# First weight chunk multiplied half by half, and three small tables given out at the second compressor chunk

## The chip, the cores and the metric

One core of a Trainium2 chip runs the whole program. The metric is the device time of one execution in microseconds (us). Its engines are TensorE (PE, with its weight loads PEld), VectorE (DVE), ScalarE (ACT), GpSimd (POOL) and SyncE (SP); each takes its instructions strictly in the order in which they were built, and waits on semaphores for the others and for transfers (DMA).

## The reference

Two decoder layers over 256 tokens of width 1024. Each layer normalises, makes one wide input projection, feeds two mixers and projects back onto the residual:

```python
def hybrid_layer(x, norm_g, w_in, ...):
    h = rms_norm(x, norm_g)
    z = h @ w_in
    (rg_x, rg_gate, q, k_c, v_c, k_s, v_s, k_w, v_w, nsa_gate, br_gate) = jnp.split(z, cuts, axis=-1)
    y_a = rg_lru(causal_depthwise_conv(rg_x, conv_w, conv_b), ..., rg_lam) * jax.nn.silu(rg_gate)
    y_b = nsa(q, k_c, v_c, k_s, v_s, k_w, v_w, br_gate, q_g, k_g, ...) * jax.nn.silu(nsa_gate)
    return x + jnp.concatenate([y_a, y_b], axis=-1) @ w_out

def rg_lru(x, w_r, b_r, w_i, b_i, lam):
    ...
    log_a = (-RG_C * r) * jax.nn.softplus(-lam)
```

The softplus of `lam` does not depend on the input x; the kernel makes it once for both layers, as a small table.

## The kernel before

Every product is done in three passes for precision: a weight chunk `raw` is split into a rounded high part `wh` (on ACT, `split`, line 167) and the rest `wl` (on DVE, line 170); the activations are likewise `hh` and `hl`. `mm3` (lines 175 to 177) adds high by high, then the two mixed products, into one PSUM bank. A product needs the chunk's `wh` for line 175's part and `wl` for one of the other two.

The weights come in chunks, in a fixed order. For layer 0: chunks 0 to 7 are `wt` (queries, and the keys of two branches; 768 columns, one eighth of the inner dimension each), chunks 8 and 9 `wc` (the compressor's keys and values), chunks 10 to 12 `wv` (values and gates), chunk 13 the first of twelve `wf`, then `wo`. SP issues the load of chunk n+4 when the subtraction that reads chunk n's `raw` buffer is done (four `raw` buffers), and SP takes its transfers in order: behind the `raw` of chunk 12 stand four small and large loads (`pes`, `w2s`, `rws`, and `yy`, which is two MB of `w1`), and behind these the `raw` of chunk 13. Chunk 0 alone is loaded and split in two halves of 384 columns; its first half is rounded on DVE (line 165), its second on ACT.

`tm1` multiplies chunk k by both token halves t and both column halves e: four PSUM banks (three named `s`, one `pp`), three matmuls each. In the same steps `first_x` scales x into `hh` and `hl` for that k, adds up squares (`sq_add`), loads the constants `cst` and the gains `ga` (k = 2), has POOL make rotary tables `cg`, `sg` from them (`tables2`, lines 247 to 252, at k = 4), has DVE copy an identity and a mask to bf16 (k = 4), and makes the `softplus` table (k = 5): two ACT operations and some seventeen small DVE operations of 128x8, of which lines 196 to 206 are one chain, each reading what the one before wrote (line 202 stands seven times).

After chunk 7, `rms1` turns the squares into the scale `rc` (PE line 310, DVE lines 311 to 320, a power on POOL, line 181) and sends it across partitions as `rp` by four tiny transfers; `cmp_scale` (ACT, line 443) needs `rp`, and the transposes of `cmp_in` (PE, line 449) need `cmp_scale`. `norm_sums` (ACT line 338, DVE lines 340 to 343, POOL line 181) and `norm_rope` (DVE lines 352 to 367) work on the two token halves. `v_out` (ACT lines 406 and 409) reads what the `wv` chunks made. Later `cmp_act` makes `hs` (line 477), which PE reads at lines 482 and 483.

The code gives instructions out in the order of the main loop; the framework's scheduler then sets each engine's order by when its own model finds them ready, so that an instruction can stand earlier or later on its engine than the code gives it out.

Of the kernel before, what the change touches and what calls it, by code (L numbers as in the profile page):

```python
# [18 lines left out]
P = 128  # L19
# [4 lines left out]
NT = S // P  # L24
# [47 lines left out]
def hybrid_trunk_kernel(ctx: ExitStack, tc: tile.TileContext, vx, wc, wt, wv, wf, wo, w1, w2, pe,  # L72
# [6 lines left out]
    V, A, G, T = nc.vector, nc.scalar, nc.gpsimd, nc.tensor  # L79
# [32 lines left out]
    for n in range(8):  # L112
        T.matmul(wb.rearrange("p (a s) -> p a s", a=2), wz[:, :P], wz[:, None].to_broadcast([P, 2, S]),
                 start=n == 0, stop=n == 7)
# [7 lines left out]
    def cview(n, p0=0, p1=P):  # L122
        a, b = CONST_COLS[n]
        return cst[p0:p1, a:b]

    ident = cview("ident")
# [5 lines left out]
    identb = cp.tile([P, P], BF16, name="identb")  # L132
    maskb = cp.tile([P, P], BF16, name="maskb")
# [40 lines left out]
    def mm3(o, lh, ll, rh, rl, start, stop):  # L174
        T.matmul(o, lh, rh, start=start, stop=False)  # L175
        T.matmul(o, lh, rl, start=False, stop=False)  # L176
        T.matmul(o, ll, rh, start=False, stop=stop)  # L177
# [12 lines left out]
    def softplus():  # L190
        sp = cp.tile([P, 6, DEPTH, 4], F32, name="sp")
        a, b = VEC_COLS["lam"]
        lam = vec[:, :, a:b]
        A.activation(sp[:, 0], lam, AF.Abs)
        A.activation(sp[:, 0], sp[:, 0], AF.Exp, scale=-1.0)
        V.tensor_scalar(sp[:, 1], sp[:, 0], 2.0, None, op0=ALU.add)
        V.reciprocal(sp[:, 1], sp[:, 1])
        V.tensor_tensor(sp[:, 1], sp[:, 1], sp[:, 0], op=ALU.mult)
        V.tensor_tensor(sp[:, 2], sp[:, 1], sp[:, 1], op=ALU.mult)
        V.tensor_scalar(sp[:, 3], sp[:, 2], 1.0 / 17, None, op0=ALU.mult)  # L200
        for c in (15, 13, 11, 9, 7, 5, 3):
            V.scalar_tensor_tensor(sp[:, 3], sp[:, 3], 1.0 / c, sp[:, 2], op0=ALU.add, op1=ALU.mult)
        V.scalar_tensor_tensor(sp[:, 3], sp[:, 3], 1.0, sp[:, 1], op0=ALU.add, op1=ALU.mult)
        V.tensor_scalar(sp[:, 4], lam, -4.0, 0.0, op0=ALU.mult, op1=ALU.max)
        V.scalar_tensor_tensor(sp[:, 4], sp[:, 3], 8.0, sp[:, 4], op0=ALU.mult, op1=ALU.add)
        V.tensor_scalar(sp[:, 5], sp[:, 4], -1.0, None, op0=ALU.mult)
        hb = cp.tile([P, DEPTH, 8], F32, name="hb")
        a = VEC_COLS["br"][0]
        V.tensor_scalar(hb, vec[:, :, a:a + 8], 0.5, None, op0=ALU.mult)
        return sp[:, 4], sp[:, 5], hb  # L210
# [5 lines left out]
    def h_split(l, h, k):  # L216
        A.activation(h[0][:, k], x_sb[:, k], AF.Copy, scale=v(l, "g", k))
        V.scalar_tensor_tensor(h[1][:, k], x_sb[:, k], v(l, "g", k), h[0][:, k].bitcast(F32),
                               op0=ALU.mult, op1=ALU.subtract)

    def sq_add(sq, k):
        if k == 0:
            A.activation(sq, x_sb[:, 0], AF.Square)
        else:
            sk = act([P, S], "tmp", 3)
            A.activation(sk, x_sb[:, k], AF.Square)
            V.tensor_tensor(sq, sq, sk, op=ALU.add)
# [4 lines left out]
    def tables(l):  # L232
        ga = act([P, NGAIN], "ga")
        nc.sync.dma_start(ga, gains[l:l + 1].to_broadcast([P, NGAIN]))
        return ga
# [22 lines left out]
    def layer(l, prev):  # L258

        L = Layer()  # L260
        steps = []

        def step(chunk, run, after=None, before=(), middle=()):
            steps.append((chunk, run, after, before, middle))
# [18 lines left out]
        def first_x(k):  # L283
            h_split(0, L.h, k)
            if k == 2:
                nc.sync.dma_start(cst, consts)
                L.ga = tables(0)
            if k == 4:
                V.tensor_copy(identb, ident)
                V.tensor_copy(maskb, cview("mask"))  # L290
                L.tabs = tables2(L.ga)
            for j in {2: [0], 3: [1, 2], 4: [3], 5: [4], 6: [5], 7: [6, 7]}.get(k, []):
                sq_add(L.sq, j)
            if k == 5:
                L.sp = softplus()

        def tm1(c, k):
            for t in range(NT):
                tok = slice(t * P, (t + 1) * P)
                for e in range(2):  # L300
                    mm3(L.acc1[t][e][:, :384], L.h[0][:, k, tok], L.h[1][:, k, tok],
                        c.hi[:, 0, e * 384:(e + 1) * 384], c.lo[:, 0, e * 384:(e + 1) * 384],
                        k == 0, k == KT - 1)
# [453 lines left out]
        F = lambda f, *a: (lambda: f(*a))  # L757
        R = lambda f, *a: (lambda c: f(c, *a))

        for k in range(KT):  # L760
# [8 lines left out]
            if l and k == 5:  # L769
# [2 lines left out]
        step(Chunk(wc[l, 0], 4, S), R(cmp_prod, 0), None, [small_loads, F(w1_load, 0), F(w1_load, 1), F(norm_sums, 0)],  # L772
             [F(norm_sums, 1)])
        step(Chunk(wc[l, 1], 4, S), R(cmp_prod, 4), cmp_scale, [],
             ([] if l else [rms2]) + [F(norm_rope, 0)])
        step(Chunk(wv[l, 0, :, :3], 3, 280), R(tm2, 0, 3), cmp_in, [],
             [F(norm_rope, 1)])
        step(Chunk(wv[l, 0, :, 3:6], 3, 280), R(tm2, 3, 3))
# [14 lines left out]
        for q in range(8):  # L793
            i, t = divmod(q, 2)
# [19 lines left out]
        for n, (kind, j) in enumerate(order):  # L814
            c = Chunk(wf[l, base[kind] + j], KT, P, dma=n >= 4)
# [14 lines left out]
    for l in range(DEPTH):  # L830
        prev, st_ = layer(l, prev)
        prev0 = prev0 or prev
        steps += st_
# [140 lines left out]
```

## Time and profile before

| what | us |
|---|---|
| median of the three timed runs | 248.19 (248.13 to 248.87) |
| the profiled execution, its own time | 248.74 |
| its span, first to last instruction | 247.0 |
| PE busy in the span | 240.0 |
| DVE busy | 195.2 |
| ACT busy | 163.7 |
| POOL busy | 44.5 |

The profile's rows give the start of an instruction, its length, its engine and line, what it writes and reads, and in square brackets the idle time before it with what ended it. A matmul's length covers a pipeline; the distance from one start to the next is what a matmul costs.

### The profile page before, as it was taken

Reading aid. Unit: us, or ns where it says so; the run is one execution under the profiler, and the core shown is the slowest. Engines: PE = TensorE matmul, PEld = TensorE weight load, DVE = VectorE, ACT = ScalarE, POOL = GpSimd, SP = SyncE. Lnnn points to the kernel's source line nnn. Section 1 sums busy time; section 2 is a strip of 40 time slices with the busy share of each in tenths; the row PEclk is TensorE's granted clock in tenths of the full one; section 3 lists DMA queues with packets and bytes.
Section 4 is the critical chain, followed back from the end, with each engine's and each line's share of the span. In section 5 each row is a group of like instructions: output and inputs, shape, how many; then the busy total and the mean of one; then the engine's idle time right before and its main releaser. Section 6 shows DMA issues by size and latency. Waiting matters only on the chain.

```text
span 247.0 us, 5194 instructions
## 1 busy us (share of the span) xinstructions
PE 240.0 (97%) x1950; PEld 222.1 (90%) x1950; DVE 195.2 (79%) x379; ACT 163.7 (66%) x414; POOL 44.5 (18%) x73
## 2 busy tenths in 40 slices
PE   8999998999999999999999999999999999999994
PEld 3999997978998899989999999987899979998993
DVE  5997698999999988654995559699997999865322
ACT  6965539799999878522872463778999998750100
POOL 0039660011600011000003044101100101110000
PEclk9999999999999999999999999999999999999998
DMA  6997999866799499842479978557669676860022
GB/s 214 363 294 268 330 404 396 261 230 170 231 338 385 129 272 323 245 150 61 133 243 328 331 247 253 183 170 239 194 189 352 220 257 165 292 226 2 3 85 85
DMA packets 17849, 57.17 MB, mean 231 GB/s; under 512 B 2464, under 2 KB 3616, under 8 KB 17312
## 3 DMA queue, kind: packets, MB, share of 16 engines
q1 hardware_dynamic: 12816, 39.86, 47.7%
q0 software_dynamic: 4864, 16.78, 21.7%
q8 instruction: 15, 0.25, 0.4%
q10 hardware_dynamic: 144, 0.20, 0.2%
q14 instruction: 10, 0.08, 0.1%
HBM read 55.78 MB, written 1.05 MB: 230 GB/s over the span
## 4 chain that ended last, share of the span: by engine, by line
PE 73%; DVE 13%; DMA 4%; ACT 3%; issue 2%; POOL 1%; SPq 0%; DVEq 0%; ACTq 0%
PE fm L175 14%; PE fm L177 13%; PE fm L176 13%; PE pp L627 4%; DVE wl L170 4%; PE s L175 3%; PE s L177 3%; PE s L176 3%; PE m L641 3%; DMA raw<-in_wv_dram 2%; PE s L587 2%; PE fm L670 2%; PE s L586 2%; DMA raw<-in_wt_dram 2%; DVE qs L390 2%
## 5 line engine op out<-in xcount | busy, mean ns | idle before, releaser
L170 DVE TENSOR_TENSOR wl<-raw,wh 128x1024 fp32r<-128x1024 f32 (+4 forms) x67 | 74.3, 1114 | 7.4 <-PE pp L176 2.4
L175 PE MATMUL fm<-hh,wh 128*128 128x256 f32 x192 | 56.9, 296 | 0.1
L177 PE MATMUL fm<-hh,wl 128*128 128x256 f32 x192 | 54.7, 285 | 1.0 <-DVE wl L170 1.0
L176 PE MATMUL fm<-hl,wh 128*128 128x256 f32 x192 | 54.6, 285 | 0.0
L167 ACT CAST wh<-raw 128x768 fp32r<-128x768 f32 (+4 forms) x34 | 30.4, 897 | 27.8 <-DMA raw<-in_wc_dram 7.8
L175 PEld LDWEIGHTS fm<-hh,wh 128*128 128x128 f32 x192 | 36.7, 191 | 1.9 <-issue 1.2
L177 PEld LDWEIGHTS fm<-hh,wl 128*128 128x128 f32 x192 | 36.7, 191 | 1.3 <-DVE wl L170 1.3
L176 PEld LDWEIGHTS fm<-hl,wh 128*128 128x128 f32 x192 | 36.7, 191 | 0.2
L599 ACT ACTIVATE pr<-s,sm 128x128 f32<-128x128 f32 (+1 forms) x64 | 26.2, 424 | 3.0 <-DVE sm L593 2.2
L175 PE MATMUL fm<-yy,wh 128*128 128x256 f32 x96 | 27.3, 285 | 0.0
L177 PE MATMUL fm<-yy,wl 128*128 128x256 f32 x96 | 26.8, 279 | 0.0
L176 PE MATMUL fm<-yy,wh 128*128 128x256 f32 x96 | 26.7, 279 | 0.0
L614 ACT ACTIVATE pr<-pr,sm 128x128 f32<-128x128 f32 (+1 forms) x64 | 23.9, 456 | 2.0 <-DVE sm L605 2.0
L156 POOL DMA_DIRECT2D wh<-in_wo_dram x16 | 8.5, 528 | 62.6 <-PE fm L177 22.6
L175 PEld LDWEIGHTS fm<-yy,wh 128*128 128x128 f32 x96 | 18.0, 188 | 0.8 <-issue 0.8
L177 PEld LDWEIGHTS fm<-yy,wl 128*128 128x128 f32 x96 | 18.0, 188 | 0.0
L176 PEld LDWEIGHTS fm<-yy,wh 128*128 128x128 f32 x96 | 18.0, 188 | 0.0
L156 POOL DMA_DIRECT2D wh<-in_wf_dram x16 | 8.8, 551 | 49.2 <-PE fm L177 22.8
L176 PE MATMUL s<-wl,hh 128*128 128x384 f32 x48 | 16.7, 348 | 0.2 <-DVE wl L170 0.2
L177 PE MATMUL s<-wh,hl 128*128 128x384 f32 x48 | 16.4, 341 | 0.0
L175 PE MATMUL s<-wh,hh 128*128 128x384 f32 x48 | 15.7, 351 | 0.0
L736 DVE TENSOR_TENSOR head<-head,fm 128x512 f32<-128x512 f32 x11 | 7.5, 686 | 9.8 <-PE fm L177 9.8
(207 smaller groups left out, 617.0 us busy)
## 6 DMA issues: line engine op xcount, KB each, us to landing
raw<-in_wf_dram SPq DMA_DIRECT2D x24, 512.0 KB, 5.1
wh<-in_wf_dram POOLq DMA_DIRECT2D x16, 512.0 KB, 5.3
raw<-in_wo_dram SPq DMA_DIRECT2D x16, 512.0 KB, 5.2
wh<-in_wo_dram POOLq DMA_DIRECT2D x16, 512.0 KB, 4.9
raw<-in_wt_dram SPq DMA_DIRECT2D x15, 384.0 KB, 4.0
yy<-in_w_dram SPq DMA_DIRECT2D x4, 1024.0 KB, 7.8
raw<-in_wc_dram SPq DMA_DIRECT2D x4, 512.0 KB, 5.3
raw<-in_wv_dram SPq DMA_DIRECT2D x4, 420.0 KB, 5.1
```

Source lines behind the costliest of these rows:

```text
L156: G.dma_start(self.wh, self.src)
L167: A.copy(hi[:, c], self.raw[:, c])
L170: V.tensor_tensor(lo[:, c], self.raw[:, c], hi[:, c].bitcast(F32), op=ALU.subtract)
L175: T.matmul(o, lh, rh, start=start, stop=False)
L176: T.matmul(o, lh, rl, start=False, stop=False)
L177: T.matmul(o, ll, rh, start=False, stop=stop)
L390: L.qk_done[t] = V.tensor_tensor(L.qs[HD:, g::2, tok], src, L.qs[:HD, g::2, tok].bitcast(F32), op=ALU.subtract)
L599: A.activation(pr[g][:, b], ov[:, b], AF.Exp, bias=sm[:, 0, 2 * g + b:2 * g + b + 1], accum_out=sm[:, 1, 2 * g + b:2 * g + b + 1])
L614: A.activation(pr[g][:, b], pr[g][:, b], AF.Copy, scale=sc_)
L627: T.transpose(pp[:, (2 * g + b) * P:(2 * g + b + 1) * P], pr[g][:, b, c * P:(c + 1) * P], ident)
L641: T.matmul(o[g * HD:(g + 1) * HD], L.vv[:, 0, b, g * HD:(g + 1) * HD], pt[:, g, b, 0:2].rearrange("p a s -> p (a s)"), start=h == b == 0, ...
L736: V.tensor_tensor(x_sb[:, m], x_sb[:, m], os_[0].rearrange("p (a s) -> p a s", a=2), op=ALU.add)
```

## The change

The products of chunk 0 are given out by column halves: for each half e, high by high for both token halves, then the `wl` products for both, then the `hl` products. Before, they went token half by token half, each with all three products of its two column halves. The bf16 identity, the mask and the softplus table, given out in the steps of chunks 4 and 5 before, are now given out by `small_tables` in the step of chunk 9, between its split and its products.

```diff
             if k == 4:
-                V.tensor_copy(identb, ident)
-                V.tensor_copy(maskb, cview("mask"))
                 L.tabs = tables2(L.ga)
...
-            if k == 5:
-                L.sp = softplus()
+
+        def small_tables():
+            V.tensor_copy(identb, ident)
+            V.tensor_copy(maskb, cview("mask"))
+            L.sp = softplus()
+
+
+        def tm1_first(c):
+            for e in range(2):
+                cols = slice(e * 384, (e + 1) * 384)
+                for q in range(3):
+                    for t in range(NT):
+                        tok = slice(t * P, (t + 1) * P)
+                        T.matmul(L.acc1[t][e][:, :384], L.h[q == 2][:, 0, tok], (c.lo if q == 1 else c.hi)[:, 0, cols],
+                                 start=q == 0, stop=False)
 
         def tm1(c, k):
+            if (l, k) == (0, 0):
+                return tm1_first(c)
...
-             ([] if l else [rms2]) + [F(norm_rope, 0)])
+             ([] if l else [rms2, small_tables]) + [F(norm_rope, 0)])
```

What the scheduler makes of it, at three places. All lines after 299 of the changed kernel have a number higher by 13.

On DVE, around the subtraction of chunk 7 (the last `wl` of 128x768). Before:

```order
L170 TENSOR_TENSOR wl<-raw,wh 128x768
L202 SCALAR_TENSOR_TENSOR sp<-sp 128x8
L227 TENSOR_TENSOR pct<-pct,tmp 128x256
L202 SCALAR_TENSOR_TENSOR sp<-sp 128x8
L203 SCALAR_TENSOR_TENSOR sp<-sp 128x8
L205 SCALAR_TENSOR_TENSOR sp<-sp 128x8
L206 TENSOR_SCALAR sp<-sp 128x8
L170 TENSOR_TENSOR wl<-raw,wh 128x768
L170 TENSOR_TENSOR wl<-raw,wh 128x1024
L311 TENSOR_SCALAR rc<-m 128x2
```

Now:

```order
L227 TENSOR_TENSOR pct<-pct,tmp 128x256
L294 CAST identb<-cst 128x128
L295 CAST maskb<-cst 128x128
L202 SCALAR_TENSOR_TENSOR sp<-sp 128x8 x6
L203 SCALAR_TENSOR_TENSOR sp<-sp 128x8
L205 SCALAR_TENSOR_TENSOR sp<-sp 128x8
L206 TENSOR_SCALAR sp<-sp 128x8
L170 TENSOR_TENSOR wl<-raw,wh 128x768
L324 TENSOR_SCALAR rc<-m 128x2
L170 TENSOR_TENSOR wl<-raw,wh 128x1024
```

The first seven or so operations of the table keep their early places; six of the seven at line 202 now stand in one row behind the subtraction of chunk 6 and ahead of that of chunk 7, where before four of them stood further up (three of these ahead of chunk 4's subtraction). The first operation on `rc` has moved ahead of chunk 8's subtraction.

On DVE, after the subtraction of chunk 9 (the second `wl` of 128x1024), where `norm_sums` reduces the squares `pt` to the sums `st`. Before:

```order
L170 TENSOR_TENSOR wl<-raw,wh 128x840
L340 TENSOR_REDUCE st<-pt 128x12 x2
L342 TENSOR_SCALAR st<-st,rc 128x8
L343 TENSOR_SCALAR st<-st,rc 128x4
L342 TENSOR_SCALAR st<-st,rc 128x8
L343 TENSOR_SCALAR st<-st,rc 128x4
L170 TENSOR_TENSOR wl<-raw,wh 128x840
```

Now:

```order
L353 TENSOR_REDUCE st<-pt 128x12
L170 TENSOR_TENSOR wl<-raw,wh 128x840
L355 TENSOR_SCALAR st<-st,rc 128x8
L356 TENSOR_SCALAR st<-st,rc 128x4
L353 TENSOR_REDUCE st<-pt 128x12
L170 TENSOR_TENSOR wl<-raw,wh 128x840
L355 TENSOR_SCALAR st<-st,rc 128x8
L356 TENSOR_SCALAR st<-st,rc 128x4
```

The sums of the first token half are finished ahead of the second half's reduction. On ACT the squares (line 338, now 351) stand between the casts of chunks 8, 9 and 10 where before all but the first stood behind that of chunk 10, and the first `vv` copy (line 406, now 419) stands ahead of the cast of chunk 13, where before it stood behind.

On DVE, where `hs` is made for the compressor. Before:

```order
L382 TENSOR_TENSOR kl<-pp,kd_122 64x2x128
L662 SCALAR_TENSOR_TENSOR cx<-xpad_72,head,cx 128x256
L390 TENSOR_TENSOR qs<-pp,qs 64x4x128
L477 SCALAR_TENSOR_TENSOR hs<-hth,m 128x160
L170 TENSOR_TENSOR wl<-raw,wh 128x1024
```

Now:

```order
L675 SCALAR_TENSOR_TENSOR cx<-xpad_72,head,cx 128x256
L395 TENSOR_TENSOR kl<-pp,kd_122 64x2x128
L490 SCALAR_TENSOR_TENSOR hs<-hth,m 128x160
L403 TENSOR_TENSOR qs<-pp,qs 64x4x128
L170 TENSOR_TENSOR wl<-raw,wh 128x1024
```

`hs` has moved ahead of the last `qs`; on ACT what it reads (`hth`, line 475, now 488) stands two copies further up, and on PE the two readers of `hs` (lines 482 and 483, now 495 and 496) stand ahead of a product of 128x512 that they stood behind. The orders of POOL and of SP are the same as before.

## Rows read from the trace of the kernel before

**Rows 1.** The page, busy time: engine, us, share of span, instructions.
```profile
PE 240.0 (97%) x1950; PEld 222.1 (90%) x1950; DVE 195.2 (79%) x379; ACT 163.7 (66%) x414; POOL 44.5 (18%) x73
```
**Rows 2.** Waits of PE: us in total, times, longest.
```profile
PE fm L177 <- DVE wl L170: 1.0, 1, 1.0
PE m L482 <- DVE hs L477: 0.5, 1, 0.5
PE fm L449 <- ACT vcb L443: 0.4, 1, 0.4
```
**Rows 3.** Timeline of PE, chunks 0, 4 and 7: start, length.
```profile
4.57 0.66 PE L175 MATMUL s<-wh,hh 128*128 128x384 f32 x1
...
6.79 0.34 PE L175 MATMUL s<-wh,hh 128*128 128x384 f32 x1
...
15.16 0.44 PE L176 MATMUL s<-wl,hh 128*128 128x384 f32 x1 [0.21 <-DVE wl L170]
...
21.44 0.33 PE L176 MATMUL s<-wl,hh 128*128 128x384 f32 x1
```
**Rows 4.** Timeline of DVE, up to chunk 7's subtraction.
```profile
6.53 0.17 DVE L196 TENSOR_SCALAR sp<-sp 128x8 f32<-128x8 f32 x1
6.73 0.20 DVE L197 RECIPROCAL sp<-sp 128x8 f32<-128x8 f32 x1
...
13.27 0.17 DVE L202 SCALAR_TENSOR_TENSOR sp<-sp 128x8 f32<-128x8 f32 x1
13.34 0.42 DVE L227 TENSOR_TENSOR pct<-pct,tmp 128x256 f32<-128x256 f32 x1
...
14.15 1.82 DVE L170 TENSOR_TENSOR wl<-raw,wh 128x768 fp32r<-128x768 f32 x2
...
17.44 0.38 DVE L202 SCALAR_TENSOR_TENSOR sp<-sp 128x8 f32<-128x8 f32 x1
17.74 0.41 DVE L227 TENSOR_TENSOR pct<-pct,tmp 128x256 f32<-128x256 f32 x1
18.08 0.37 DVE L202 SCALAR_TENSOR_TENSOR sp<-sp 128x8 f32<-128x8 f32 x1
18.48 0.32 DVE L203 SCALAR_TENSOR_TENSOR sp<-sp 128x8 f32<-128x8 f32 x1
...
19.18 0.53 DVE L206 TENSOR_SCALAR sp<-sp 128x8 f32<-128x8 f32 x1
19.62 0.95 DVE L170 TENSOR_TENSOR wl<-raw,wh 128x768 fp32r<-128x768 f32 x1
```
**Rows 5.** Timeline of DVE, from chunk 8 to chunk 13's subtraction.
```profile
20.77 1.23 DVE L170 TENSOR_TENSOR wl<-raw,wh 128x1024 fp32r<-128x1024 f32 x1 [0.20 <-ACT wh L167]
...
24.70 1.03 DVE L170 TENSOR_TENSOR wl<-raw,wh 128x840 fp32r<-128x840 f32 x1 [0.43 <-ACT wh L167]
25.65 1.80 DVE L340 TENSOR_REDUCE st<-pt 128x12 f32<-128x768 f32 x2
...
31.12 1.02 DVE L352 TENSOR_TENSOR pt<-s,st 128x384 f32<-128x384 f32 x2 [2.19 <-POOL st L181]
...
37.76 1.23 DVE L170 TENSOR_TENSOR wl<-raw,wh 128x1024 fp32r<-128x1024 f32 x1
```
**Rows 6.** Timeline of POOL.
```profile
16.52 1.91 POOL L247 TENSOR_TENSOR cg<-ga,cst 128x96 f32<-128x96 f32 x2 [15.49 <-DMA ga<-in_gains_dram]
...
22.21 0.72 POOL L181 TENSOR_TENSOR rc<-rc,mhalf 128x2 f32<-128x2 f32 x1
...
27.82 5.50 POOL L181 TENSOR_TENSOR st<-st,mhalf 128x12 f32<-128x12 f32 x2 [2.23 <-DVE st L343]
```
**Rows 7.** Timeline of ACT around chunk 13's cast.
```profile
35.47 1.05 ACT L167 CAST wh<-raw 128x1024 fp32r<-128x1024 f32 x1 [3.14 <-DMA raw<-in_wf_dram]
36.64 0.47 ACT L406 ACTIVATE vv<-pp,rc 128x256 f32<-128x256 f32 x1
```
**Rows 8.** Issue of chunk 13's raw at 24.82: KB, us from issue to landing.
```profile
raw<-in_wf_dram SPq DMA_DIRECT2D x1, 512.0 KB, 10.6
```

## The prediction
> **What bounds the kernel now.** I read the page first: PE is busy for 240.0 of 247.0 us [rows 1], so the time can only move where PE stands still. The list of PE's waits then names every such place after the start: 1.0 us for the subtraction of chunk 13, 0.5 for `hs`, 0.4 for `vcb` [rows 2] and 0.21 for the subtraction of chunk 4 [rows 3], some 2.1 us in all, and all before 53 us. After `hs` the list shows no wait of PE. So the question is when PE passes the read of `hs`: from there to the end some 194 us of products follow without a hole, and a shift there is a shift of the end. Up to there PE is tied to DVE by the subtractions, and the timelines of DVE, POOL and ACT [rows 4 to 7] say which of them arrives late.
>
> **The first chunk by halves.** Nothing is added: the same twelve matmuls. Before, the first six take from 4.57 to 6.79 [rows 3], among them waits for the second half's parts; by halves, PE has two matmuls to do on each part as it comes, and it ends the chunk some tenths sooner (my estimate from that stretch is 0.2 to 0.3, no row shows it). But PE loses it again at chunk 4: there it waits 0.21 us for the subtraction [rows 3], and whoever comes sooner waits longer. I therefore count the halves at nothing for the end; what covers them is the wait of chunk 4, and if that wait were gone they would be worth their 0.2 to 0.3.
>
> **What leaves the stretch ahead of chunk 4.** Three of the seven operations of line 202 move behind chunk 6's subtraction. Each took 0.07 us of DVE, as the one at 13.27 with the next start at 13.34 [rows 4], together 0.21 or 0.22. Chunk 4's subtraction starts at 13.93 in place of 14.15, and PE's wait there ends 0.22 earlier, at 14.94. The identity and mask copies barely move; they stand behind chunk 6's subtraction in place of ahead of it and cost the same.
>
> **What piles up ahead of chunk 7.** Nine dependent operations now stand in a row (six of line 202, then 203, 205, 206), where before the last four did. Spread out, an operation hid its answer time behind a large one; in a row each waits for the one before. Four ran in a row before, from 18.08 to 19.62 [rows 4], 0.385 us each, and the one of line 202 took 0.40 to the next start. The five that join cost 5 x 0.40 = 2.00; the places they leave gave 0.22 ahead of chunk 4 and 0.37 between (0.07 for one like that at 13.27, and 0.30 for the one at 17.44 [rows 4]). So chunk 7's subtraction starts at 19.62 + 2.00 - 0.59 = 21.03 and ends at 21.98. The price is uncertain: without POOL at work the same chain ran at 0.20 from start to start, 6.53 to 6.73 [rows 4]. At 0.20 for all nine, the subtraction would start at 19.62 + 1.00 - 0.59 - 4 x 0.185 = 19.29. I take the high value: POOL starts its tables at 16.52 as before [rows 6], since its gains come by the same transfer, and it is at them during the whole row. Above it, 0.53 (the length of line 206) for all nine would give 22.3.
>
> What the trace shows here is that a 128x8 operation takes 0.17 before POOL starts and 0.32 to 0.38 while POOL works [rows 4, 6]. The Trainium skill, page "SBUF — State Buffer", section "Who interferes with whom", says that a DVE instruction with two SBUF inputs and a GpSimd instruction that reads SBUF exclude each other for the whole instruction. By that rule this change moves its work to the wrong place, since the row comes to lie in POOL's window from end to end; the trace agrees with 0.17 against 0.38, and the sum by the rule is the 21.03 above, that without it the 19.29.
>
> PE has done its first product of chunk 7 by then and wants the second at 21.44 - 0.22 = 21.22. It gets it at some 22.03 (0.05 for the signal is my allowance), so PE stands 0.8 us there and is 0.59 behind the kernel before. No PE wait stood there before.
>
> **Who else is behind that row.** (1) The first operation on `rc` follows chunk 7's subtraction: 22.0, and POOL's power on it then starts at some 22.15, where before it started at 22.21 because POOL was held by its tables until then [rows 6]. So `rp` and `vcb` come as before, and PE, 0.59 late, reaches the transposes behind `vcb` without most of the wait of 0.35 to 0.4 [rows 2]: it is then some 0.2 behind, no longer 0.59. (2) Chunk 8's subtraction starts at 22.05 in place of 20.77 [rows 5] and ends at 23.2 in place of 22.0. With it go the SP issues behind it, in order: the `raw` of chunk 12, the four small loads with `yy`, the `raw` of chunk 13, each about 1.2 us later. (3) Chunk 9's cast now waits for the first squares of chunk 7's sums, so its subtraction ends at 25.15, 0.9 later than before.
>
> **The norm chain.** DVE stood 2.19 us for POOL's first power [rows 5]. Ahead of POOL's start now stands one reduction fewer (half of 1.80 [rows 5]) and two small operations fewer (0.2), against the 0.9 of chunk 9 and with the 0.43 of idle ahead of chunk 10's subtraction [rows 5] gone: 27.82 + 0.9 - 0.9 - 0.2 - 0.4 gives about 27.2. The two powers take 5.50 together and run on from there, so the rotary work starts 0.6 earlier than 31.12, and DVE is free for chunk 13's subtraction at about 37.1 in place of 37.76 [rows 5].
>
> **The wait for chunk 13.** Before, its `raw` landed at 24.82 + 10.6 = 35.4 [rows 8], its cast ended at 36.5, and DVE came at 37.76: DVE was last by 1.2 us. Now the landing comes up to 1.2 later, at 36.6 at the latest if the queue's speed is the same, and the cast stands behind the first `vv` [rows 7], which waits for PE: 36.64 + 0.1 to 0.2, and it takes some 0.4 (0.47 long, overlapping the next). So the cast runs from 37.1 to 38.05, the subtraction from 38.1 to 39.25, and PE goes on at 39.3 in place of 39.03. The cast is now the last, behind `vv`, by 0.5 us over the landing; the price of the whole pile-up has shrunk to 0.27 us.
>
> **`hs`.** It moves ahead of the last `qs` (0.7 us of DVE) and its input ahead of two copies on ACT. Even with DVE and ACT 0.5 us late in this stretch (ACT takes one more step ahead of its casts), `hs` is there when PE comes, and the product that PE now does behind it needs nothing that is late. PE's 0.46 us wait (0.5 in the list [rows 2]) goes: 0.27 - 0.46 = -0.2 at the high price. At the low price PE comes to chunk 13 in front: `rp` comes about a microsecond sooner (POOL's tables end sooner too, near 20.7, and `rc` then waits for PE's sums of squares at 21.1), `vv` is 0.6 earlier, chunk 13 goes on at 38.65, and the sum is -0.4 - 0.46, about -0.85. I take -0.3, nearer to the high price, whose row has the same neighbour at work.
>
> **Rivals.**
> (a) The row of nine runs at the price without POOL. For it: POOL's first table operation is held by a subtraction of DVE and will end sooner now that chunk 6's subtraction comes sooner. Against it: lengths of 0.32 to 0.38 in that stretch [rows 4]. Result -0.85.
> (b) The transfers take over. Chunk 13's `raw` already needs 10.6 us from issue to landing [rows 8], behind two MB; issued 1.2 us later it may meet more of the later traffic. It decides from a landing at 37.1 on; from there PE pays us for us. At 38.3 (2.9 after the old landing) PE goes on at 40.5, 1.5 late, and less the 0.46 of `hs`, the kernel is 1.0 slower, 249.2. Against it: the issue moves by 1.2, and 35.4 + 1.2 leaves 0.5 to spare; so the transfers behind the two MB must also run slower than before.
> (c) The change does nothing that can be seen: the halves are lost at chunk 4, the pile-up of 0.6 goes into the waits of `vcb` and chunk 13, and `hs` is late by as much as DVE is (0.5 us), so that its wait stays. Result +0.2.
>
> **How the numbers follow.** The sum stands against the profiled execution: 248.74 - 0.3 = 248.4. That execution is 0.55 above the median of the three timed runs, 248.19; the same step from the median gives 247.9. A difference under 0.3%, 0.74 us, is about what cannot be told from no change here. The forecast, between -0.6 and +0.1: 0.5. Rival (a), 247.3: 0.2, of which I give 0.17 to more than 0.74 gained. Rival (c), 248.4: 0.18. Rival (b): 0.12, of which 0.1 past 0.74. Faster 0.18, same 0.71, slower 0.11. The range holds (a) down to 247.3 and (c) with the smaller half of (b), up to 248.8.
>
> **What would show it.** PE's wait for chunk 4 ends near 14.94 and starts sooner. A new PE wait of 0.6 to 0.8 us for `wl` stands near 22.0; without it, or with one under 0.3, the price of the nine was too high, and rival (a) is right. The `raw` of chunk 13 is issued near 26.0 and lands by 36.6. PE goes on with chunk 13 near 39.3, and the wait of line 482's successor for `hs` is gone. If chunk 13's cast waits for its transfer and not for `vv`, it is (b); if PE still waits 0.4 for `hs`, it is (c). The prediction is wrong altogether if PE waits after 53 us, where the trace before shows none.

## The result, and the profile after

The changed kernel is slower. Its first four executions gave 250.15, 250.31, 251.99 and 252.75 us, median 251.15, against 248.41 (248.13 to 248.87) for the kernel before on the same chip: a ratio of 1.0119, 95% interval 1.0087 to 1.0150. Five more, later, gave 250.26 to 251.87 and a ratio of 1.0108 (1.0091 to 1.0125). The prediction was 247.9, at most 248.8, with 0.11 for slower. The execution profiled took 250.15 and has a span of 248.4, where the profiled one of before has 247.0; so the traces show 1.4 us of a loss that is 2.7 in the median, and the wider spread is part of what has to be explained. No execution of the changed kernel above 250.3 was profiled.

The page gives the same picture as [rows 1], PE being busy 97% of the span. First its busy row, then the list of PE's waits (us in total, times, longest) of the changed kernel; from line 299 on its line numbers are 13 higher than before's.

```profile
PE 240.6 (97%) x1950; PEld 221.9 (89%) x1950; DVE 195.7 (79%) x379; ACT 163.8 (66%) x414; POOL 42.6 (17%) x73
```
```profile
PE fm L175 <- ACT wh L167: 0.9, 1, 0.9
PE m L495 <- DVE hs L490: 0.7, 1, 0.7
PE m L517 <- DVE kcd L513: 0.6, 1, 0.6
PE fm L177 <- DVE wl L170: 0.3, 1, 0.3
PE s L176 <- DVE wl L170: 0.3, 1, 0.3
```

Beside [rows 2], the wait for `vcb` has gone, the one for `hs` has grown from 0.5 to 0.7, and a wait for `kcd` is new. On PE's timeline these are the places:

```profile
15.00 0.44 PE L176 MATMUL s<-wl,hh 128*128 128x384 f32 x1
...
21.72 0.44 PE L176 MATMUL s<-wl,hh 128*128 128x384 f32 x1 [0.27 <-DVE wl L170]
...
38.10 0.39 PE L175 MATMUL fm<-hh,wh 128*128 128x256 f32 x1 [0.95 <-ACT wh L167]
...
39.36 0.39 PE L177 MATMUL fm<-hh,wl 128*128 128x256 f32 x1 [0.31 <-DVE wl L170]
...
53.42 0.30 PE L495 MATMUL m<-w2s,hs 128*32 128x64 f32 x2 [0.74 <-DVE hs L490]
...
60.77 0.22 PE L517 MATMUL m<-cst,kcd 32*128 32x32 f32 x1 [0.55 <-DVE kcd L513]
```

Up to the fourth of them the kernel does in the main what was foreseen: chunk 4 at 15.00 (14.94 predicted), chunk 7 late by 0.28 against [rows 3] (0.59 predicted), chunk 13 at 39.36 (39.3 predicted, 39.03 before). The loss on PE appears behind it. DVE around chunk 7, beside [rows 4], and below it POOL's tables:

```profile
17.54 2.21 DVE L202 SCALAR_TENSOR_TENSOR sp<-sp 128x8 f32<-128x8 f32 x6
19.79 0.17 DVE L203 SCALAR_TENSOR_TENSOR sp<-sp 128x8 f32<-128x8 f32 x1
19.99 0.17 DVE L205 SCALAR_TENSOR_TENSOR sp<-sp 128x8 f32<-128x8 f32 x1
20.19 0.17 DVE L206 TENSOR_SCALAR sp<-sp 128x8 f32<-128x8 f32 x1
20.71 0.96 DVE L170 TENSOR_TENSOR wl<-raw,wh 128x768 fp32r<-128x768 f32 x1 [0.35 <-ACT wh L167]
21.59 0.15 DVE L324 TENSOR_SCALAR rc<-m 128x2 f32<-128x2 f32 x1
21.66 1.22 DVE L170 TENSOR_TENSOR wl<-raw,wh 128x1024 fp32r<-128x1024 f32 x1
```
```profile
18.89 0.60 POOL L249 TENSOR_TENSOR ga<-ga 128x192 f32<-128x192 f32 x1
19.45 0.28 POOL L250 TENSOR_TENSOR ga<-ga 32x48 f32<-32x48 f32 x1
19.69 0.21 POOL L251 TENSOR_TENSOR ga<-ga,cst 32x16 f32<-32x16 f32 x1
19.87 0.21 POOL L252 TENSOR_TENSOR ga<-ga,cst 32x16 f32<-32x16 f32 x1
```

The nine stand in a row: six at 0.375 from start to start on the mean (0.34 to 0.56 for the first five, 0.24 for the sixth) and three at 0.20. Each of the first six ends 0.02 to 0.03 us after an operation of POOL (17.91 after 17.88, and so on to 19.75 after 19.72), so they take as long as POOL's operations beside them; the price falls from 19.55 on, when POOL's operations have become as short as 0.21 to 0.28, and not only when POOL's tables end at 20.08. Chunk 7's subtraction ends at 21.67, before at 20.57 [rows 4]. SP issues chunk 11's load 0.03 us after that end, in both kernels, and everything behind it on SP moves along, chunk 13's load among it (the rows' times were 20.60 and 24.82 before):

```profile
21.70 1.53 SPq L148 DMA_DIRECT2D raw<-in_wv_dram  x2
...
25.71 5.88 SPq L148 DMA_DIRECT2D raw<-in_wf_dram  x4
```

The stretch from 20 to 30 us shows what is moved less by it. The last two columns are the DMA engines' busy share and the GB/s; first the kernel before, then the changed one:

```profile
20.00:25.00 5.00, 5.00 (x36) 5.00 (x35) 3.71 (x8) 3.40 (x6) 4.55 (x7) 1.00 0.75 241
25.00:30.00 5.00, 5.00 (x44) 5.00 (x43) 3.92 (x8) 2.72 (x7) 2.77 (x3) 1.00 0.93 321
```
```profile
20.00:25.00 5.00, 4.73 (x32) 4.48 (x31) 3.97 (x10) 3.09 (x6) 2.89 (x4) 1.00 0.63 200
25.00:30.00 5.00, 5.00 (x44) 5.00 (x44) 4.65 (x10) 2.84 (x6) 3.88 (x5) 1.00 0.99 297
```

It is (241 - 200 + 321 - 297) x 5 = 325 KB less, 0.8 us at the 403 to 411 GB/s at which the engines then run full in both kernels (share 0.98 to 1.08) from 30 to 40 us; the engines' busy share is lower only up to 25 us. POOL meanwhile does the opposite. It issues its own two loads of 512 KB, chunks 17 and 18, 1.56 us sooner; before, then after:

```profile
33.28 1.15 POOL L156 DMA_DIRECT2D wh<-in_wf_dram  x2
```
```profile
27.23 4.53 POOL L181 TENSOR_TENSOR st<-st,mhalf 128x12 f32<-128x12 f32 x2 [1.12 <-DVE st L356]
31.72 1.15 POOL L156 DMA_DIRECT2D wh<-in_wf_dram  x2
```

So loads that are needed late go ahead of, or among, loads that are needed soon. Chunk 15's `raw`, issued between 28 and 29 us in either kernel, takes 9.0 us from issue to landing before and 12.2 after (columns: KB, us to landing):

```profile
raw<-in_wf_dram SPq DMA_DIRECT2D x1, 512.0 KB, 9.0
```
```profile
raw<-in_wf_dram SPq DMA_DIRECT2D x1, 512.0 KB, 12.2
```

On ACT two things come together, the new order (`vv` ahead of chunk 13's cast) and that landing. After, beside [rows 7]:

```profile
36.65 0.47 ACT L419 ACTIVATE vv<-pp,rc 128x256 f32<-128x256 f32 x1 [4.32 <-PE pp L177]
37.02 1.03 ACT L167 CAST wh<-raw 128x1024 fp32r<-128x1024 f32 x1
...
39.84 0.35 ACT L393 CAST kd<-pp 64x256 fp32r<-64x256 f32 x1
...
41.28 1.05 ACT L167 CAST wh<-raw 128x1024 fp32r<-128x1024 f32 x1
```

and the same two last steps before:

```profile
38.64 0.36 ACT L380 CAST kd<-pp 64x256 fp32r<-64x256 f32 x1
...
39.89 1.04 ACT L167 CAST wh<-raw 128x1024 fp32r<-128x1024 f32 x1
```

`vv` stands at the same time in both, PE being done with its products at the same time. But the first `kd` comes 1.20 us later, and chunk 15's cast 1.39. The chain of waits that the profile draws for the changed kernel runs through that cast, straight from the transfer:

```profile
28.96 12.24 DMA raw<-in_wf_dram
41.24 0.04 issue
41.28 1.05 ACT wh L167
```

But a chain follows whatever came last, by however little. From the start of ACT's step ahead of it (40.60) to this cast it is 0.68 us, before 0.49; to chunk 14's cast at 38.72, whose load landed at 38.64, it is 0.59, before 0.36. So these two landings held ACT back by 0.19 and 0.23 us.

From there ACT and DVE hand work to each other, past DVE's first row maximum `sm` of the attention, up to ACT's first squaring of `rr`, a step of the recurrent mixer. Before, then after:

```profile
45.66 0.69 DVE L593 TENSOR_REDUCE sm<-s 128x4 f32<-128x512 f32 x1
61.00 0.65 ACT L682 ACTIVATE tmp<-rr 128x512 f32<-128x512 f32 x1
```
```profile
46.51 0.69 DVE L606 TENSOR_REDUCE sm<-s 128x4 f32<-128x512 f32 x1
62.41 0.65 ACT L695 ACTIVATE tmp<-rr 128x512 f32<-128x512 f32 x1
```

The squaring is 1.41 late, which is the whole difference of the spans: 0.85 up to `sm`, 0.56 between `sm` and the squaring. In three other profiles with this order on ACT, in which no cast waits for a load, 9.42 to 9.44 us lie between `vv` and `sm`; here it is 9.86, which is the 0.42 of the two landings. So some 0.4 of the 1.4 goes with the late loads in this execution, and the rest with the order. In 17 of the 18 profiles of this study 185.8 to 186.2 us lie between the squaring and the end of the span: what is lost is lost ahead of this row. PE's list of waits does not tell it, having grown from 2.1 only to 2.8 us.

### The profile page after: what moved, and what is told of

It is laid out like the page before. It is cut to its first block, busy times and chain, and to the rows that moved or that the text cites. A ratio compares the mean times of both kernels' runs of the same rounds, so it can differ in the third digit from the quotient of the medians.

```text
span 248.4 us, 5195 instructions
## 1 busy us (share of the span) xinstructions
PE 240.6 (97%) x1950; PEld 221.9 (89%) x1950; DVE 195.7 (79%) x379; ACT 163.8 (66%) x414; POOL 42.6 (17%) x73
## 4 chain that ended last, share of the span: by engine, by line
PE 71%; DMA 11%; DVE 8%; ACT 6%; issue 2%; SPq 0%; ACTq 0%
PE fm L175 13%; PE fm L176 12%; PE fm L177 12%; DMA raw<-in_wf_dram 5%; PE pp L640 4%; PE s L176 3%; PE s L177 3%; PE s L175 3%; PE m L654 3%; DMA head<-in_vx_dram 3%; PE s L599 2%; PE s L600 2%; ACT wh L167 2%; PE fm L683 2%; DMA raw<-in_wc_dram 2%
## 5 line engine op out<-in xcount | busy, mean ns | idle before, releaser
L176 PE MATMUL s<-wl,hh 128*128 128x384 f32 x45 | 15.4, 342 | 0.3 <-DVE wl L170 0.3
L177 PE MATMUL s<-wh,hl 128*128 128x384 f32 x45 | 15.1, 335 | 0.0
L83 ACT COPY pt<-pp 128x512 f32<-128x512 f32 x24 | 13.4, 594 | 2.1 <-PE pp L640 2.1
```

The source lines that it names most:

```text
L83: A.copy(o, i)
```

## The experiments

Each ratio is to the kernel before on the same chip, with its 95% interval.

### Which part of the change does it

Three kernels take the change apart: the halves alone; the halves with the two rounding copies in their new place; the tables without the halves (run twice). The changed kernel was run again beside them.

Against the kernel before, the halves alone add `tm1_first` and its call. Against the changed kernel, the second kernel has

```
+            if k == 5:
+                L.sp = softplus()
...
         def small_tables():
             V.tensor_copy(identb, ident)
             V.tensor_copy(maskb, cview("mask"))
-            L.sp = softplus()
```

and the tables alone

```
-            if (l, k) == (0, 0):
-                return tm1_first(c)
```

> The kernel before with only the first chunk's products by halves. It isolates the half of the change that the tables run left out. Theory (lost at chunk 4's wait): no change from the kernel before, 248.4 to 249.0 where that one gives 248.8; chunk 0 products from 4.7 us, and PE's wait for chunk 4's low part ends at 15.1 to 15.2 as before; chunk 13's raw is issued at 24.8 and the cast of chunk 13 stands ahead of the first vv. Rival (the halves carry part of the loss, since the changed kernel measured 1.2% against 0.6% for the tables alone): 249.3 to 250.0.

> The halves, and only the rounded identity and the rounded mask given out at the second compressor chunk; the softplus ops stay where they were in the kernel before. ACT's order is then that of the kernel before, PE's too but for chunk 0. Theory (the softplus ops in their new place carry the loss: they pile up ahead of chunk 7, make SP's issues late by 0.9 us and put vv ahead of chunk 13's cast): no loss, 248.2 to 249.0, PE's first wait from chunk 13 on ends by 39.1. Rival (any late op ahead of chunk 7 costs, or the halves do): 249.5 to 250.3.

> The kernel before with the tables given out at chunk 9, the products of chunk 0 as before. Theory A (a late ACT: the first vv stands ahead of chunk 13's cast, and everything ACT and DVE do from 40 to 60 us comes later) and theory B (the pile-up of nine small DVE operations ahead of chunk 7, which puts off PE there and the transfers behind it) both expect the whole loss here, 250 to 253 us, since the halves were counted at nothing; if the halves carry the loss, this is 248.4.

> The changed kernel without the halves, which had six runs (1.0057), against 1.0108 and 1.0119 for the changed kernel. If the halves change nothing once the tables have moved and that was the scatter of the loads: 250.3 to 251.5, ratio 1.007 to 1.012. If they add to the loss: 249.7 to 250.3, ratio 1.004 to 1.007.

> The changed kernel as it stands, in more runs than the four it had. The halves alone measured as no change and the tables alone 0.57% slower, so if the two parts don't work together it is 249.8 to 250.6, 0.4 to 0.8% slower than the kernel before, with a spread of 2 us or more. If the halves matter once the tables have moved (the first four runs gave 1.2%): 251 to 252. In either case chunk 7's subtraction ends after 21.4 us, the raw load of chunk 11 is issued within 0.1 us of that end, and the first row maximum is followed by ACT's first squaring of rr in 15.8 to 16.0 us.

Measured: the halves alone 248.20, 1.0004 (0.9991 to 1.0018); with the copies moved too 248.35, 1.0009 (0.9992 to 1.0025); the tables alone 250.07, 1.0057 (1.0038 to 1.0076), and the second time 250.27, 1.0066 (1.0046 to 1.0086); the changed kernel again 251.37, 1.0108. So the halves are worth nothing by themselves, the two copies cost nothing, and the loss comes with the nine softplus operations. Together with them the halves do seem to add: 1.0062 on the mean of two without, 1.0108 and 1.0119 with. With the halves 6 of 9 executions are above 250.7, without them 3 of 12. What the halves do there was not shown; a later run bears on it.

### The row of nine, and the order on ACT

Three repairs on DVE and ACT, each a dependency that sets an order and no more: the softplus operations behind the norm's sums ("gap"), the first `rc` operation behind chunk 8's subtraction ("early subtraction"), the first `vv` behind chunk 13's cast ("cast first").

```
-            V.scalar_tensor_tensor(sp[:, 3], sp[:, 3], 1.0 / c, sp[:, 2], op0=ALU.add, op1=ALU.mult)
+            with tc.issue_after(behind) if c == 13 else nullcontext():
+              V.scalar_tensor_tensor(sp[:, 3], sp[:, 3], 1.0 / c, sp[:, 2], op0=ALU.add, op1=ALU.mult)
...
+            with tc.issue_after(ch[8].lo_ins.ins) if l == 0 else nullcontext():
+                V.tensor_scalar(rc[:, 0, :2], p_ss[:, :2], 1.0 / D, EPS, op0=ALU.mult, op1=ALU.add)
...
+                with tc.issue_after(ch[13].hi_ins.ins) if l == t == 0 else nullcontext():
+                    A.activation(L.vv[:, t].rearrange("p b d -> p (b d)"), L.acc2[t][:, :2 * P], AF.Copy,
+                                 scale=L.rc[:, 1, t:t + 1])
```

Here `behind` is the norm's last sum, `lo_ins` the subtraction of a chunk, `hi_ins` its cast.

Cast first alone, twice:

> The changed kernel with one order set by hand: on ACT the first vv copy behind chunk 13's cast, as before the change. The scheduler then gives all orders after 44 us as in the kernel before; the pile-up stays. Theory A: 248.0 to 248.6, the loss is gone. Theory B: 250 to 252, since the pile-up, PE's wait at chunk 7 and the later transfers are all there.

> The kernel of vv_behind_cast once more, which had few runs there, from 249.0 to 251.5, and in its profile a load of chunk 13 that took 12.5 us. If the scatter of that load's landing is the kernel's own (its loads are issued 0.7 us later into a queue that is full from 25 us on): again 249.5 to 250.5 with a spread of 2 us. If that batch was an accident: 248.6 to 249.2, as the run that has the softplus ops in the gap.

Measured: 250.24 (249.00 to 251.47), 1.0064 (1.0040 to 1.0088), and 250.21 (249.01 to 252.09), 1.0071 (1.0043 to 1.0099). The order of before on ACT alone does not bring the time back. In the first of these profiles ACT stands for the transfers at two casts, chunk 13's (5.47 us, where it was 3.14 before [rows 7]) and chunk 14's:

```profile
38.10 1.04 ACT L167 CAST wh<-raw 128x1024 fp32r<-128x1024 f32 x1 [5.47 <-DMA raw<-in_wf_dram]
...
40.67 1.05 ACT L167 CAST wh<-raw 128x1024 fp32r<-128x1024 f32 x1 [0.61 <-DMA raw<-in_wf_dram]
```

Chunk 13's load was issued at 25.55 and took 12.5 us there, chunk 14's 13.9.

The gap alone, and both:

> The changed kernel with the last nine operations of the softplus table put behind norm_sums on DVE, where it waits for POOL; every other order is that of the changed kernel, the vv copy ahead of chunk 13's cast among them. Theory B: 247.5 to 248.4, since the pile-up and the delay of the transfers are gone. Theory A: 249.5 to 250.5, since vv still waits for PE ahead of the cast; only what PE is earlier (0.3 to 0.5 us) comes off.

> Both orders set by hand: the nine operations behind norm_sums, and vv behind chunk 13's cast. Theory A: 247.5 to 248.2, under the kernel before by the 0.2 us at chunk 4 and a norm chain that starts earlier; the same as the run with vv alone, within 0.5. Theory B: 247.5 to 248.4, and at least 2 us under the run with vv alone.

Measured: the gap 249.98 (248.83 to 251.62), 1.0040 (1.0019 to 1.0061); both 249.06, 1.0012 (0.9991 to 1.0032), no longer told from before. The gap's profile also showed why SP did not come back: DVE stood 2.18 us for the first `rc` operation's input, with chunk 8's subtraction queued behind it, so chunk 13's load was still issued at 25.91. Hence the early subtraction:

> The changed kernel with its nine softplus ops put behind the norm's sums and the first rc op put behind chunk 8's subtraction, both on DVE; vv still stands ahead of chunk 13's cast, and the later orders on ACT and PE are those of the changed kernel. Both theories: chunk 8's subtraction starts at 20.5 to 20.9, and SP issues chunk 13's raw at 24.6 to 25.0 (25.7 in the changed kernel). Theory A (the late issues carry the loss): 248.5 to 249.0. Theory B (the order on ACT and DVE behind vv carries it): 249.6 to 250.2, with the waits for ACT's cx and DVE's xpad of 0.5 us at 49 to 50 us and PE's wait for kcd of about 0.5 us still there.

> As the run above (softplus behind the norm's sums, rc behind chunk 8's subtraction), and the first vv behind chunk 13's cast on ACT as well, which gives ACT and PE the order of the kernel before nearly everywhere. If the two causes together are the whole loss: 247.8 to 248.7, level with the kernel before or up to 0.4% better, chunk 13's raw issued at 24.6 to 25.0, PE on after chunk 13 at 38.0 to 39.0. If something else in the change carries it (the new place of the two rounding copies, the halves): 249.2 to 250.

> The changed kernel with the first vv behind chunk 13's cast on ACT (the order of the kernel before there) and the first rc op behind chunk 8's subtraction; the nine softplus ops still pile up ahead of chunk 7. The difference to the run with the softplus ops in the gap (248.61) is then the pile-up alone. Theory A (the pile-up holds back chunk 7's subtraction, so the DMA engines run dry at 21 to 22 us, and chunk 13 lands about 1 us later, with no slack on ACT): 249.3 to 250.3, chunk 13's raw issued at 25.3 to 25.7, its cast waiting for the transfer and starting after 36.2. Theory B (only the order on ACT costs): 248.3 to 248.9. In either case the stretch from the first row maximum on DVE to ACT's first squaring of rr is 15.2 to 15.4 us, as in every kernel with the order of before, and not 15.9.

Measured: gap and early subtraction 249.29, 1.0037 (1.0022 to 1.0052); with cast first 248.61, 1.0013 (0.9999 to 1.0027); the last, cast first and early subtraction with the row of nine ahead of chunk 7 again, 250.27, 1.0053 (1.0029 to 1.0078). Chunk 13's load was issued at 24.52, 24.60 and 26.11.

Three readings. First, with the loads early, the order alone is 249.29 - 248.61 = 0.7 us, on one chip. It acts at two places, and each measures the same in every profile: from the start of the first `vv` to the first `kd` it is 2.95 us with `vv` ahead of the cast and 1.99 to 2.09 with the cast ahead, when chunk 14's cast does not wait for its load; from the first row maximum `sm` to the squaring of `rr` it is 15.88 to 15.92 us in the seven profiles with the new order and 15.22 to 15.35 in the ten others that keep ACT's work. Not all of the first piece is lost, since `vv` need not wait for the cast where it goes ahead. The second piece is this exchange, after; `cx` now stands ahead of the second `kd` on ACT, and each engine waits once for the other (0.54, 0.67), where before DVE's wait for `cx` was 0.21 and ACT had none:

```profile
49.52 0.60 ACT L673 ACTIVATE cx<-xpad,head 128x256 f32<-128x256 f32 x1 [0.54 <-DVE xpad L672]
```
```profile
50.16 0.48 DVE L675 SCALAR_TENSOR_TENSOR cx<-xpad,head,cx 128x256 f32<-128x256 f32 x1 [0.67 <-ACT cx L673]
```

Second, with the order of before, the row of nine alone is 1.0053 against 1.0013, with executions from 248.56 to 251.54 where the other has 247.66 to 249.35. The row of nine widens the spread; the order does not (248.79 to 250.30).

Third, the later issue of chunk 13's load is not enough for the loss. With the row in the gap, the early subtraction moves that issue from 25.91 to 24.52, and with cast first from 25.64 to 24.60; the ratios stay (1.0040 and 1.0037, 1.0012 and 1.0013), and only the highest execution falls, from 251.62 to 250.30 and from 251.31 to 249.35. The gap's kernel issues the loads of chunks 13 to 15 and POOL's two within 0.2 us of the changed kernel's times and has 1.0040, not 1.0108; of the loads behind chunk 10 it is chunk 11's alone that it issues clearly sooner (19.63, 21.70). So the row may cost by what is still to be moved when the later loads come. No run isolates that, and bytes alone don't tell: the halves alone moved 165 KB less than before from 20 to 30 us and lost nothing.

### Whose loads collide

That the spread goes with the landings can be read where a long execution was profiled. In the second profile of the tables alone, of 251.25 us, chunk 14's load took 12.7 us and its cast waited for it, which in the first, of 249.83 us, it did not (11.3 us):

```profile
40.00 1.05 ACT L167 CAST wh<-raw 128x1024 fp32r<-128x1024 f32 x1 [0.73 <-DMA raw<-in_wf_dram]
```

From `vv` to the first row maximum it is then 10.47 us in place of 9.54. To tell the late issue on SP from the early issue on POOL, one more power operation of 8 columns was put on POOL between the norm's two, its result unused. No other engine's order changes.

```
+            if l == 0 and t == 1:
+                rsqrt_small(act([P, 8], "rcd"), st[:, 0, :8], 8)
```

> As pileup_cast_first (250.27, ratio 1.0053), with one more power op of 8 columns on GpSimd behind the norm's two, its result unused; by 4.53 us for two of 12 columns it takes about 1.5 us, and GpSimd's two loads of 512 KB are issued at 33.5 to 34 us and not at 32.2. All other engines keep their orders. Theory (these loads run ahead of chunk 13's and 14's and lengthen them): chunks 13 and 14 land up to 1 us sooner, the scatter shrinks, ratio 1.000 to 1.004. Rival (the late issue on SP alone): ratio still 1.004 to 1.008, the spread still 2.5 to 3 us.

> The changed kernel with the same extra power op on GpSimd. Theory (GpSimd's early loads): the runs at 251 to 252.8 become fewer, 249.6 to 250.4, ratio 1.003 to 1.007, what the order behind vv costs being left (the stretch from the first row maximum to the squaring of rr stays at 15.8 to 16.0 us). Rival: 251.0 to 251.9, ratio 1.009 to 1.013, as without the op.

> The kernel with the softplus ops in the gap, the early subtraction and the order of before on ACT (ratio 1.0013), with the same extra power op on GpSimd. Its load of chunk 13 landed without harm, its cast of chunk 14 waited 0.27 us for a load. Theory: 247.9 to 248.4, ratio 0.997 to 1.000, the first kernel that might beat the kernel before. Rival: no change, ratio 1.000 to 1.003.

POOL in the changed kernel with that operation:

```profile
29.90 1.62 POOL L181 TENSOR_TENSOR rcd<-st,mhalf 128x8 f32<-128x8 f32 x1
31.50 2.25 POOL L181 TENSOR_TENSOR st<-st,mhalf 128x12 f32<-128x12 f32 x1
33.72 1.15 POOL L156 DMA_DIRECT2D wh<-in_wf_dram  x2
```

Measured: row of nine, cast first 249.24 (248.61 to 250.09), 1.0027 (1.0010 to 1.0043), from 1.0053; the changed kernel 250.47 (250.08 to 250.69), 1.0072 (1.0055 to 1.0089), from 1.0108; with all repairs 248.50, 1.0001 (0.9989 to 1.0014), from 1.0013. The ratio falls in all three kernels, though work was added to an engine; only in the changed kernel are the intervals apart, and there just (1.0091 to 1.0125 against 1.0055 to 1.0089), and the two of a pair were run on different chips. In the first two kernels no execution is above 250.7, where without the operation 3 of 12 and 6 of 9 were. In the changed kernel's profile chunk 15's load, issued between 29 and 30 us, now takes 10.4 us and not 12.2, and no cast waits for a load:

```profile
raw<-in_wf_dram SPq DMA_DIRECT2D x1, 512.0 KB, 10.4
```

This profiled execution is no faster for it (250.23, beside 250.15 and 250.26): the gain is in the long executions that are missing. And the sooner landing is not in every pair of profiles. With all repairs chunk 15's load went from 11.8 to 9.0 us, but with the row of nine and cast first the loads of chunks 13 to 15 took 10.9, 11.1 and 11.6 us with the operation and 10.2, 11.0 and 11.5 without; there the profiles are of the longest of twelve executions (250.09) and of one of the shorter ones (249.24). So the collision with POOL's loads is borne out by the times of one kernel and by some of the profiles, and is not shown for each.

The changed kernel with POOL's loads late (1.0072) lies where the tables alone lie with them early (1.0062). So the added loss beside the halves may be this collision, met more often; the runs fit that, and don't prove it.

| row of nine | early subtraction | order on ACT | POOL's loads | ratio |
|---|---|---|---|---|
| ahead of chunk 7 | no | changed | early | 1.0108, 1.0119 |
| ahead of chunk 7 | no | changed | late | 1.0072 |
| ahead of chunk 7 | no | as before | early | 1.0064, 1.0071 |
| ahead of chunk 7 | yes | as before | early | 1.0053 |
| ahead of chunk 7 | yes | as before | late | 1.0027 |
| gap | no | changed | early | 1.0040 |
| gap | no | as before | early | 1.0012 |
| gap | yes | changed | early | 1.0037 |
| gap | yes | as before | early | 1.0013 |
| gap | yes | as before | late | 1.0001 |

By steps: POOL's loads 0.36, 0.26 and 0.12%, in the order of the table; the order on ACT and DVE 0.24 and 0.28% with the row in the gap (1.0072 - 1.0027 = 0.45% with POOL's loads late, but there the early subtraction comes in too); the row of nine 0.40% with POOL's loads early (1.0053 against 1.0013) and 0.26% with them late (1.0027 against 1.0001). The shares depend on the path, and with intervals of 0.13 to 0.31% to each side the single ones are rough. What is firm is the ends: with the row in the gap and the cast first the kernel, halves included, is no longer told from before, and neither repair alone does that.

### A try to win at the place

If ACT alone were the bound from 46 to 61 us, taking work off it should pay. In the kernel before, POOL does the first layer's `cx` products:

```
-            A.activation(cx[:, j], xp[:, 4:], AF.Identity, scale=v(l, "cw", 12 + j), bias=v(l, "cb", j))
+            if l == 0:
+                G.tensor_scalar(cx[:, j], xp[:, 4:], v(l, "cw", 12 + j), v(l, "cb", j), op0=ALU.mult, op1=ALU.add)
+            else:
+                A.activation(cx[:, j], xp[:, 4:], AF.Identity, scale=v(l, "cw", 12 + j), bias=v(l, "cb", j))
```

> The kernel before, with the first layer's four cx ops (128x256, 0.58 to 0.60 us each on ACT) given to GpSimd; two of them stand between 48 and 56 us. If ACT is the bound from 46 to 61 us, as 4.92 of 5 and 4.97 of 5 us of busy time say, its first squaring of rr comes up to 1.1 us sooner and the time is 247.2 to 248.0. If DVE or PE is the bound there, or GpSimd's use slows DVE by as much: 248.3 to 249.5.

Measured: 249.90, 1.0040 (1.0026 to 1.0054), slower. The squaring of `rr` comes at 60.77, 0.23 sooner than before, though the row maximum comes 0.67 sooner, and from there to the end it is 186.9 us, the one exception above. With less work on ACT the stretch from the row maximum to the squaring is 15.78 us, longer than the 15.34 of before: ACT's busy time is not the bound by itself. That the hand-over between ACT, DVE and PE is, is argued and not shown, since the scheduler moved other steps too. No kernel here beats the kernel before.

## Why the prediction was wrong, point by point

- **The halves: right at the end (1.0004), lost at another wait.** PE started chunk 1 0.33 us sooner (7.50, before 7.83), but its first `wl` product there stood behind chunk 1's subtraction (8.40, the subtraction ending at 8.35), and chunk 2 started at 9.92, before at 9.91. So nothing was left for the wait of chunk 4 to take, which the prediction said covers them.
- **Chunk 4: right.** Its product starts at 15.00, with 14.94 predicted.
- **The row of nine: the right mechanism, mis-sized, and luck in the sum.** The row took 2.82 us (17.54 to 20.36), with 3.54 predicted: the price was not 0.385 to 0.40 throughout, but that of POOL's operation beside it, and fell to 0.20 as these became short. The Trainium skill, page "SBUF — State Buffer", section "Who interferes with whom", says that a DVE instruction with two SBUF inputs contends with a GpSimd instruction that reads SBUF; the ends 0.02 to 0.03 us behind POOL's agree. DVE then stood 0.35 us ahead of chunk 7, which was in no sum. It is 0.34 to 0.35 in all nine profiles with the row there, and what holds DVE is not known. With it chunk 7's subtraction ended at 21.67, only 0.3 from the predicted 21.98. PE's wait was 0.27 and not 0.8, and behind `vcb` PE was level again (32.38 in both kernels), with 0.2 late predicted.
- **SP's queue and chunk 13: right.** The load was issued at 25.71 (26.0), landed at 36.4 (36.6 at the latest), `vv` came first at 36.65, PE went on at 39.36 (39.3).
- **The norm chain: a term mis-sized, and a consequence left out.** POOL's powers started at 27.23, as predicted, but took 4.53 and not 5.50. So POOL's loads came not 0.6 but 1.56 us sooner, into the stretch that SP's late loads had been moved to. The prediction followed SP's queue past the moved row and never asked what a faster POOL would start.
- **Rival (b): a part of the cause, set at the wrong chunk.** It watched the landing of chunk 13, from 37.1 on. That landing held, at 36.4. The loads of chunks 14, 15 and 16, issued behind it, took 11.7, 12.2 and 12.5 us in place of 10.9, 9.0 and 7.4. In the profiled execution they held ACT back by 0.42 us in all; in the long executions it was more, as far as the profiles of long executions of two other kernels show.
- **`hs`, and the 194 us of products "without a hole" behind it: the step that failed.** The list of PE's waits of before has nothing after 53 us [rows 2], and the prediction took PE for the bound from chunk 13 on: with PE only 0.27 late there, `hs` "is there when PE comes", and its 0.46 comes off. But the parts of ACT and DVE were paced by each other from `vv` on: the first `kd` came 1.20 late, `hs` 0.45 (52.59 to 53.04). So PE's wait did not go but grew to 0.74, and `kcd` became a wait of 0.55 at 60.77, which the prediction itself named as the sign that it is wrong altogether. Counted on PE alone, the 0.95 us that the first `kd` comes later behind `vv`, in every profile with this order, was hidden; counted on ACT, a part of it stayed, and the exchange up to the squaring added 0.56.

Slower was given 0.11; a late ACT, a worse exchange behind it and late loads together were in none of the cases.

## What to carry to other kernels

A list of waits that names one busy engine says where that engine stood, not which engine sets the pace; before a late step is counted as absorbed, follow it on every engine that has work queued behind it, to the row from which all versions run alike. A chain that runs through a transfer says that it came last, not what it cost: compare the step that it released with the same step in a version that did not wait. Filling a gap on DVE with small dependent operations also delays the buffers behind them, and with these the loads; and an engine that gets faster starts its own loads sooner, which can push back the loads that are needed first. When a kernel's times begin to spread, look at the landing of its loads.

## What the runs showed of the hardware

- **A POOL operation that starts just before a DVE subtraction, or inside one, is longer.** Before, POOL's first power of 12 columns started at 27.82 with chunk 11's subtraction (27.90, 1.02 us) beside it, and took 3.27; its second took 2.26, and in the changed kernel the two took 4.53. On two columns the power took 0.72 before [rows 6] and 1.56 beside chunk 8's subtraction. In the changed kernel the power was 0.68 us on its way when chunk 11's subtraction started (27.91), and neither was longer for it: the subtraction took its usual 1.02, the powers 4.53. So it was the POOL operation that had just started, or started inside, that took longer, and the subtraction never did: 3.27 in all four profiles with the first meeting and 2.30 in the fourteen others.
- **A load of 512 KB on SP took 7.4 to 14.1 us** from issue to landing, over chunks 13 to 16 of all profiles: the same bytes, issued at other times beside other loads. Chunk 15's took 12.2 us in the changed kernel, and 10.4 with POOL's loads 2.00 us later.
- **A small DVE operation beside a longer POOL operation ended when that did.** In the row of nine the second to fifth 128x8 operation took 0.31 to 0.52 us beside POOL operations of 0.38 to 0.60 and ended 0.02 to 0.03 behind them; beside those of 0.21 such an operation took 0.17.
